# Splitting expert weights a whole slab at a time, with the products of the low parts queued one slab later

## The chip, the cores and the metric

The kernel runs on one core of one Trainium2 chip. The metric is the device time of one execution in microseconds (us); smaller is better. Three runs of the kernel before have a median of 2082.76 us (2081.35 to 2083.7).

## What is computed

The reference is a two-layer trunk over 256 latent tokens of width 1024, with 256 context tokens beside them. Layer 0 has a pooling and attention mixer and a dense SwiGLU, layer 1 a gated DeltaNet mixer and a SwiGLU of eight experts, of which each token uses two. The change lies in the experts:

```python
D_MODEL = 1024; SEQ = 256; N_EXPERTS = 8; TOP_K = 2; D_EXPERT = 3584

def swiglu(h, w1, w3, w2):
    return (jax.nn.silu(h @ w1) * (h @ w3)) @ w2

logits = jnp.matmul(t, router, preferred_element_type=jnp.float32)
top_v, top_i = lax.top_k(logits, TOP_K)
gates = jax.nn.softmax(top_v, axis=-1)
combine = jnp.sum(jax.nn.one_hot(top_i, N_EXPERTS) * gates[..., None], axis=1)
for e in range(N_EXPERTS):
    y = y + combine[:, e:e + 1] * swiglu(t, w1[e], w3[e], w2[e])
```

All data are fp32. The expert weights, 3 x 8 x 1024 x 3584 numbers, are 352 MB, and the kernel reads all of them.

## The kernel before

**Products in two parts.** TensorE multiplies in a reduced format (F32R), so each operand is split: a high part, which is the operand copied into F32R, and a low part, the rest. `split_w` (L235) does this for 1024 columns of weights: ScalarE (ACT) writes the high part `whi` (L238), VectorE (DVE) subtracts it from the raw weights and writes `wlo` (L239). Each of the two has a ring of three tiles in the pool `wp`. The same function serves every weight matrix of the kernel, also in the first 1090 us, before the experts. A product is then high by high, low by high and high by low (`mm3w`, L243 to L246).

**Slabs.** Weights come from HBM in slabs of 128 x 2048 numbers, 1 MB each, one DMA per slab, all issued by SyncE (SP) from `load` (L232) or `slab` (L1524). The experts have 8 x 7 units of work (expert, chunk of 512 hidden columns), and a unit has six slabs: four for `up` (two halves of the contraction for w1 and w3 each) and two for `down`, so 336 slabs. A slab waits in one of nine raw buffers, three from the pool `rawp` and six (`NR`) from `rw2`, taken in rotation; four more slabs use spare tiles (`spare`) that later hold other data. A raw buffer is free again when both halves of its slab are split, so the last reader is the subtraction at L239.

**Large and small experts.** The expert of index 0 and the three with the most tokens are large (128 slots, high and low part of the tokens as two weights of TensorE: three matmuls per block of 128 x 512, L244 to L246). The four with the fewest tokens are small (64 slots, high and low part side by side in 128 columns: two matmuls per block, L1804 and L1806 in `up`, L1859 and L1861 in `down`). So a slab of a large expert has 12 matmuls of 512 columns and one of a small expert 8. `units` (L1923) interleaves a chunk of a small and a chunk of a large expert.

**Order of one unit.** `up(c)` (L1789) does the first two slabs, then `turn` of the previous unit (L1821: the activations are transposed, or for a small expert folded at L1828, split by ACT and DVE at L1830 to L1841), then the other two slabs, and then reads out its sums (L1813 to L1818). After it comes `down` of the previous unit (L1844). The products of a half slab stand in the code directly behind its split. The order in the code is a priority: for each engine the language draws up the order of its instructions when the program is built, and at run time every engine works its list strictly in that order, waiting on semaphores.

**Where it starts and ends.** The first slabs are requested while layer 1 still runs. `route_large` and `route_small` gather the tokens of an expert. `finish` (L1866) spreads an expert's output over the tokens. After the last unit come the last norm and the output (L1998 to L2002).

```python
        n = turn[0] - 1 - sum(j < turn[0] for j in spare)
        return load(src, rawp if n % (NR + 3) < 3 else rw2)
```

Of the kernel before, what the change touches and what calls it, by code (L numbers as in the profile page):

```python
# [18 lines left out]
P = 128  # L19
# [149 lines left out]
def trunk(ctx, tc, I, out, dbg=None, stop=None):  # L169
# [12 lines left out]
    def psA():  # L182
        return pa.tile([P, 512], F32, tag="A", name="psA")
# [304 lines left out]
    with ExitStack() as mx:  # L488
# [131 lines left out]
        def softmax(qt, kv):  # L620

            lat = qt < 2
            k0 = 0 if lat else SEQ
            nk = T - k0
            r64 = slice(64 * kv, 64 * kv + 64)
            if kv == 0:
                prs = []
                for tag in ("whi", "wlo"):
                    pr = wp.tile([P, 1024], F32, tag=tag, name="pr")
                    prs += [pr[:, 0:512], pr[:, 512:1024]]  # L630
            else:
                prs = [w2() for g in range(4)]
            nm = sp.tile([P, 4], F32, tag="nm", name="nm")
            l4 = sp.tile([P, 4], F32, tag="l4", name="l4")
            mx_ = sp.tile([P, 4, 2], F32, tag="mx", name="mx")
            for g in range(4):
                h = 4 * kv + g
                n1 = nm[:, g:g + 1]
                ps = psA()
                TE.matmul(ps[:, :nk], qT[g][r64, qt * P:(qt + 1) * P], kT[0][r64, k0:], start=True, stop=True)  # L640
                if lat:
                    V.tensor_tensor_reduce(ps[:, :SEQ], ps[:, :SEQ], amask[:, qt, :], 1.0, -3e38, OP.add, OP.max,
                                           mx_[:, g, 0:1])
                V.tensor_reduce(mx_[:, g, 1:2], ps[:, nk - SEQ:nk], axis=AX.X, op=OP.max)
                V.tensor_scalar(n1, mx_[:, g, 1:2], -0.125, nsink[:, h:h + 1], op0=OP.mult, op1=OP.min)
                if lat:
                    V.tensor_scalar(n1, mx_[:, g, 0:1], -0.125, n1, op0=OP.mult, op1=OP.min)
                S.activation(prs[g][:, :nk], ps[:, :nk], AF.Exp, bias=n1, scale=0.125, accum_out=l4[:, g:g + 1])
                yield True
            es = sp.tile([P, 4], F32, tag="es", name="es")  # L650
            V.tensor_add(es, sinkb[:, 4 * kv:4 * kv + 4], nm)
            S.activation(es, es, AF.Exp)
            V.tensor_add(l4, l4, es)
            V.reciprocal(l4, l4)
            for g in range(4):
# [943 lines left out]
    def m2():  # L1599
        return tm.tile([P, 512], F32, tag="m2", name="m2")  # L1600
# [163 lines left out]
    def route_small(x):  # L1764
# [11 lines left out]
        for h in range(2):  # L1776
# [2 lines left out]
                TE.transpose(ps[:, col(i)], f(oh[:, i % 2, 2 * h + i // 2].rearrange("p a s -> p (a s)")), ident)  # L1779
            S.activation(oTs[:, 2 * h:2 * h + 2].rearrange("p e t s -> p (e t s)"), ps, AF.Copy)  # L1780

    def expert(w, into, gain, first=False):


# [3 lines left out]

        def up(c, ahead=None, raws=None, between=None):  # L1789
            h1, h3 = psA(), psA()  # L1790
            for kh in range(2):
                if kh and between:
                    between()
                raw1, raw3 = raws or [slab(w(n, c, kh)) for n in ("moe1", "moe3")]
                raws = None
                for q in range(2):
                    if ahead:
                        next(ahead, None)
                    for raw_, ps in ((raw1, h1), (raw3, h3)):
                        wh, wl = ready.pop(0) if ready else split_w(raw_[:, q * 1024:(q + 1) * 1024])  # L1800
                        ks = [(4 * kh + 2 * q + kk, slice(kk * 512, (kk + 1) * 512)) for kk in range(2)]
                        if small_:
                            for k, s in ks:
                                TE.matmul(ps, into.x(k), wh[:, s], start=k == 0, stop=False)  # L1804
                            for k, s in ks:
                                TE.matmul(ps, into.x(k), wl[:, s], start=False, stop=k == KD - 1)  # L1806
                        else:
                            for k, s in ks:
                                mm3w(ps, into.x[:, k, 0, :], into.x[:, k, 1, :], wh[:, s], wl[:, s], k == 0,
                                     k == KD - 1)  # L1810
            if small_:
                hs = [m2(), m2()]
                S.activation(hs[0], h1, AF.Copy)  # L1813
                S.activation(hs[1], h3, AF.Copy)
                return hs
            sg = m2()
            S.activation(sg, h1, AF.Silu)
            V.tensor_mul(sg, sg, h3)  # L1818
            return sg

        def turn_(sg):  # L1821
            ps = psA()
            gh = mo.tile([P, 512], F32R, tag="gh", name="gh")
            if small_:
                for i in range(2):
                    for b in range(4):
# [17 lines left out]
        def down(c, ghl, between=None):  # L1844
            gh, gl = ghl
            if not y:
                y.extend([psB(), psB()])
            for fh_ in range(2):
                if fh_ and between:
                    between()  # L1850
                raw_ = slab(w("moe2", c, fh_))
                for q in range(2):
                    b = 2 * fh_ + q
                    wh, wl = split_w(raw_[:, q * 1024:(q + 1) * 1024])
                    start, stop = c == 0 and b == 0, c == NCH - 1 and b == 3
                    halves = [slice(n * 512, (n + 1) * 512) for n in range(2)]
                    if small_:
                        for n, s in enumerate(halves):
                            TE.matmul(y[n], gh[:, col(b)], wh[:, s], start=start, stop=False)  # L1859
                        for n, s in enumerate(halves):  # L1860
                            TE.matmul(y[n], gh[:, col(b)], wl[:, s], start=False, stop=stop)  # L1861
                    else:
                        for n, s in enumerate(halves):
                            mm3w(y[n], gh[:, col(b)], gl[:, col(b)], wh[:, s], wl[:, s], start, stop)

        def finish():  # L1866
            yhl_ = mo.tile([P, 2, D], F32R, tag="hl", name="yhl_")
# [67 lines left out]
    last = None  # L1935
    ending, aheads = [], []
    count = NE * NCH
    for n, (into, c) in enumerate(units()):
        if n == 0:
            sg = into.up(c, ahead, raws0)  # L1940
            for _ in ahead:
                pass
            gains()
            sort()
            aheads = [route_small(xs_)]
            next(aheads[0])
        else:
            got = []
            sg = into.up(c, between=lambda: got.append(last.turn(last.sg)))
            if ending:  # L1950
                next(ending.pop(), None)
            if n == count - 1:
                last.down(last.c, got.pop(), lambda: got.append(into.turn(sg)))
            else:
                last.down(last.c, got[0])
            if last.c == NCH - 1:
                ending.append(last.finish())
                next(ending[0])
        if n == 1:
            sorted_experts()  # L1960
        if into in large and c == 0 and into is not large[-1]:
# [4 lines left out]
                if next(aheads[0], 0) == 0:  # L1966
                    aheads.pop(0)
        last = into
        last.sg, last.c = sg, c
    last.down(last.c, got[0])  # L1970
    for _ in last.finish():
        pass

# [2 lines left out]
    with tc.If(n_most > CAP):  # L1976
        with tc.For_i(0, NE) as e:
# [11 lines left out]
            expert(lambda n, c, s: I[n][bass.ds(e, 1), c, s].rearrange("o p f -> (o p) f"), into,  # L1989
                   lambda t: one[:, t, 1:2])  # L1990
            for c in range(NCH):
                into.down(c, into.turn(into.up(c)))
            for _ in into.finish():
                pass

# [24 lines left out]
```

## Time and profile before

| what | value |
|---|---|
| runs, median | 2082.76 us (2081.35 to 2083.7) |
| the profiled execution, its own time | 2079.91 us |
| its span, first to last instruction | 2078.1 us |
| mean granted TensorE clock | 0.978 of full speed |
| read from HBM in all | 516.67 MB |

The profile is of one execution. "Busy" is the time in which an engine executes; DMA share is the mean busy share of the 16 DMA engines. PEld is TensorE's weight load, which runs beside its matmuls; the matmuls' ends are modelled, so that consecutive ones overlap in the profile and their distance, start to start, says what one costs. In the list of waits, "A <- B: us, times" is the idle time of an engine just before instruction A that B ended. The tile names are the program's, and `psA` and `psB` are the two PSUM pools.

### The profile page before, as it was taken

How to read it: one execution, taken by the hardware profiler on the slowest of the kernel's cores; microseconds unless marked ns; L12 is line 12 of the kernel's file. 1: busy time of each engine (PE TensorE's matmuls, PEld its weight loads, DVE VectorE, ACT ScalarE, POOL GpSimd, SP SyncE). 2: the span in 40 equal slices, each digit the busy share in tenths (PEclk: the TensorE clock that was granted, in tenths of full speed). 3: DMA queues.
4: the chain of work that ended last, by engine and by line, in shares of the span. 5: the costliest groups of instructions: out<-in, count | busy, mean ns of one | idle time of the engine just before them, and what ended most of it. 6: DMA issues, size and time to landing. Idle time of an engine off the chain costs nothing. (4 is left out here: it accounts for less than half of the span.)

```text
span 2078.1 us, 29337 instructions
## 1 busy us (share of the span) xinstructions
PE 1941.4 (93%) x10425; PEld 1523.2 (73%) x10425; DVE 1601.4 (77%) x2522; ACT 1372.7 (66%) x2231; POOL 117.8 (6%) x163
## 2 busy tenths in 40 slices
PE   6999999999999899899979999999999999999996
PEld 3747677788888778898857877676767676766774
DVE  3475755576778687786659998889898888889897
ACT  5254654455666656645448887778777778777775
POOL 0000000000011214213000000000000000000000
PEclk9999999999999999999979999999999999999999
DMA  9352577744545233113147999898989899999993
GB/s 354 142 194 82 192 261 261 268 158 158 192 159 187 96 139 132 41 63 121 64 183 276 374 386 363 338 348 356 387 348 357 331 383 369 355 364 352 366 381 121
DMA packets 74074, 519.70 MB, mean 250 GB/s; under 512 B 9456, under 2 KB 9616, under 8 KB 11584
## 3 DMA queue, kind: packets, MB, share of 16 engines
q1 hardware_dynamic: 72864, 515.51, 65.4%
q0 software_dynamic: 1056, 2.24, 0.5%
q8 instruction: 84, 1.38, 0.3%
q14 instruction: 70, 0.57, 0.1%
HBM read 516.67 MB, written 1.05 MB: 249 GB/s over the span
## 5 line engine op out<-in xcount | busy, mean ns | idle before, releaser
L239 DVE TENSOR_TENSOR wlo<-raw,whi 128x1024 fp32r<-128x1024 f32 x878 | 1042.9, 1227 | 174.7 <-ACT whi L238 164.8
L238 ACT ACTIVATE whi<-raw 128x1024 fp32r<-128x1024 f32 x878 | 903.1, 1056 | 245.2 <-PE psA L245 98.6
L246 PE MATMUL psA<-wlo,xl 128*128 128x512 f32 x448 | 179.1, 400 | 8.4 <-DVE wlo L239 8.4
L244 PE MATMUL psA<-whi,xl 128*128 128x512 f32 x448 | 182.7, 409 | 2.5 <-ACT whi L238 1.6
L245 PE MATMUL psA<-whi,xl 128*128 128x512 f32 x448 | 176.4, 394 | 0.0
L1806 PE MATMUL psA<-wlo,xs 128*128 128x512 f32 x448 | 148.1, 412 | 14.4 <-DVE wlo L239 14.4
L1804 PE MATMUL psA<-whi,xs 128*128 128x512 f32 x448 | 147.3, 408 | 7.9 <-ACT whi L238 7.9
L244 PE MATMUL psB<-whi,gh 128*128 128x512 f32 x312 | 124.3, 399 | 0.1
L245 PE MATMUL psB<-whi,gl 128*128 128x512 f32 x312 | 123.4, 395 | 0.0
L246 PE MATMUL psB<-wlo,gh 128*128 128x512 f32 x312 | 112.0, 407 | 4.5 <-DVE wlo L239 4.1
L1806 PEld LDWEIGHTS psA<-wlo,xs 128*128 128x128 f32 x448 | 76.1, 188 | 52.3 <-DVE wlo L239 40.7
L787 PE MATMUL psB<-fx,whi 128*128 128x512 f32 x308 | 111.9, 402 | 0.7 <-DVE w L446 0.7
L787 PE MATMUL psA<-fx,whi 128*128 128x512 f32 x308 | 111.2, 399 | 0.6 <-DVE w L793 0.6
L246 PEld LDWEIGHTS psA<-wlo,xl 128*128 128x128 f32 x448 | 84.7, 189 | 35.2 <-DVE wlo L239 17.4
L1804 PEld LDWEIGHTS psA<-whi,xs 128*128 128x128 f32 x448 | 80.9, 189 | 35.8 <-ACT whi L238 21.2
L244 PEld LDWEIGHTS psA<-whi,xl 128*128 128x128 f32 x448 | 84.5, 189 | 26.0 <-ACT whi L238 10.5
L245 PEld LDWEIGHTS psA<-whi,xl 128*128 128x128 f32 x448 | 84.8, 189 | 17.1 <-DVE xl L1744 0.3
L788 PE MATMUL psB<-fx,wlo 128*128 128x256 f32 x352 | 91.7, 281 | 0.0
L788 PE MATMUL psA<-fx,wlo 128*128 128x256 f32 x352 | 91.6, 281 | 0.0
L1861 PE MATMUL psB<-wlo,gh 128*128 128x512 f32 x224 | 77.2, 426 | 15.0 <-DVE wlo L239 15.0
L264 POOL TENSOR_TENSOR rstd<-rstd,mhalf 128x1 f32<-128x1 f32 x17 | 13.5, 798 | 1358.4 <-DVE ss L1554 1002.4
L249 PE MATMUL psB<-jx,whi 128*128 128x256 f32 x256 | 78.1, 305 | 3.2 <-DVE glast L446 3.2
(519 smaller groups left out, 3853.0 us busy)
## 6 DMA issues: line engine op xcount, KB each, us to landing
raw<-in_moe SPq DMA_DIRECT2D x336, 1024.0 KB, 7.2
raw<-in_ffn SPq DMA_DIRECT2D x66, 1024.0 KB, 4.9
raw<-in_l_mod SPq DMA_DIRECT2D x48, 1024.0 KB, 6.4
raw<-in_w_qkvz SPq DMA_DIRECT2D x24, 1024.0 KB, 4.9
raw<-in_w_out SPq DMA_DIRECT2D x8, 1024.0 KB, 4.9
raw<-in_w_in SPq DMA_DIRECT2D x5, 1024.0 KB, 9.8
w<-in_l_post POOLq DMA_DIRECT2D x8, 256.0 KB, 4.9
x<-in_x SPq DMA_DIRECT2D x2, 512.0 KB, 5.0
```

The source lines that it names most:

```text
L238: S.activation(hi, src, AF.Copy)
L239: V.tensor_sub(lo, src, f(hi))
L244: TE.matmul(ps, ah, bh, start=start, stop=False)
L245: TE.matmul(ps, al, bh, start=False, stop=False)
L246: TE.matmul(ps, ah, bl, start=False, stop=stop)
L249: TE.matmul(ps, ah, bh, start=start, stop=False)
L264: G.tensor_tensor(r, r, mhalf[:, 0:n], op=OP.pow)
L787: TE.matmul(ps2, wh[:, c], hilo[:, k], start=k == 0, stop=False)
L788: TE.matmul(ps2[:, 0:SEQ], wl[:, c], hi[:, k], start=False, stop=False)
L1804: TE.matmul(ps, into.x(k), wh[:, s], start=k == 0, stop=False)
L1806: TE.matmul(ps, into.x(k), wl[:, s], start=False, stop=k == KD - 1)
L1861: TE.matmul(y[n], gh[:, col(b)], wl[:, s], start=False, stop=stop)
```

## The change

- `split_w` allocates its high and low part as one tile of `wp` (tag "w", three buffers) in place of two tiles with rings of their own. Memory stays as it was. The attention tile `pr` follows.
- In the experts, a new `split_slab` splits all 2048 columns with one ACT and one DVE instruction. The high part goes to a buffer of `rawp` (three of 2048 columns), the low part to one of `wp` (three of 2048 columns).
- Raw slabs now use the six buffers of `rw2` alone; the spare tiles stay.
- `later` holds back the products of the low parts: in the order of the code, those of a slab come behind the products of the high part of the next slab. The reading out of a unit's sums (`hidden`) and the start of `finish` are held back with them.
- The first two slabs of the first unit keep the old way (two halves of 1024).

```diff
     def split_w(src, n=1024):
-        hi = wp.tile([P, n], F32R, tag="whi", name="whi")
-        lo = wp.tile([P, n], F32R, tag="wlo", name="wlo")
+        both_ = wp.tile([P, 2, n], F32R, tag="w", name="w")
+        hi, lo = both_[:, 0], both_[:, 1]
...
-        n = turn[0] - 1 - sum(j < turn[0] for j in spare)
-        return load(src, rawp if n % (NR + 3) < 3 else rw2)
+        return load(src, rw2)
+
+    def split_slab(src):
+
+        hi = rawp.tile([P, 2048], F32R, tag="raw", name="whi")
+        lo = wp.tile([P, 2048], F32R, tag="w", name="wlo")
+        S.activation(hi, src, AF.Copy)
+        V.tensor_sub(lo, src, f(hi))
+        return hi, lo
...
-        spare[NR + 6 + j] = lambda tag=tag: mo.tile([P, 2048], F32, tag=tag, name="raw")
+        spare[NR + 3 + j] = lambda tag=tag: mo.tile([P, 2048], F32, tag=tag, name="raw")
...
+    pending = []
+
+    def later(*work):
+
+        for g_ in pending[:]:
+            g_()
+        pending[:] = work
...
+                for name, ps in (("moe1", h1), ("moe3", h3)):
+                    wh, wl = split_slab(slab(w(name, c, kh)))
+                    ks = [(4 * kh + i, slice(i * 512, (i + 1) * 512)) for i in range(4)]
+                    for k, s in ks:
+                        high(ps, wh, k, s)
+
+                    def lows_(ps=ps, wl=wl, ks=ks):
+                        for k, s in ks:
+                            low(ps, wl, k, s)
+
+                    later(lows_)
...
+            pending.append(hidden)
...
-                raw_ = slab(w("moe2", c, fh_))
-                for q in range(2):
-                    b = 2 * fh_ + q
-                    wh, wl = split_w(raw_[:, q * 1024:(q + 1) * 1024])
...
+                wh, wl = split_slab(slab(w("moe2", c, fh_)))
+                parts_ = [(2 * fh_ + q, n, slice(q * 1024 + n * 512, q * 1024 + (n + 1) * 512))
+                          for q in range(2) for n in range(2)]
+                for b, n, s in parts_:
+                    TE.matmul(y[n], gh[:, col(b)], wh[:, s], start=c == 0 and b == 0, stop=False)
+                    if not small_:
+                        TE.matmul(y[n], gl[:, col(b)], wh[:, s], start=False, stop=False)
+
+                def lows_(wl=wl, parts_=parts_):
+                    for b, n, s in parts_:
+                        TE.matmul(y[n], gh[:, col(b)], wl[:, s], start=False, stop=c == NCH - 1 and b == 3)
+
+                later(lows_)
...
             if last.c == NCH - 1:
-                ending.append(last.finish())
-                next(ending[0])
+                pending.append(lambda last=last: begin_end(last))
```

## Rows read from the trace of the kernel before

**Rows 1.** The page, part 1: busy time and share of the span.
```profile
PE 1941.4 (93%) x10425; PEld 1523.2 (73%) x10425; DVE 1601.4 (77%) x2522; ACT 1372.7 (66%) x2231; POOL 117.8 (6%) x163
```

**Rows 2.** Windows: length, busy us by engine, then PEclk, DMA share, GB/s.
```profile
0.00:1090.00 1090.00, 1020.73 (x6325) 829.68 (x6326) 726.99 (x1618) 598.14 (x1299) 116.71 (x161) 0.97 0.46 164
1130.00:2040.00 910.00, 859.61 (x3818) 646.89 (x3817) 809.25 (x803) 720.88 (x857) 0.00 (x0) 1.00 0.93 361
1828.00:1858.00 30.00, 28.36 (x126) 20.90 (x125) 26.12 (x26) 23.71 (x28) 0.00 (x0) 1.00 1.00 407
```

**Rows 3.** Groups of instructions by shape, 1130 to 2040 us.
```profile
L239 DVE TENSOR_TENSOR wlo<-raw,whi 128x1024 fp32r<-128x1024 f32 x628 | 734.4, 1222 | 62.3 <-ACT whi L238 58.6 <-PE psB L1861 0.5
L238 ACT ACTIVATE whi<-raw 128x1024 fp32r<-128x1024 f32 x629 | 641.2, 1056 | 94.7 <-PE psA L245 61.3 <-PE psB L245 10.0 <-DVE wlo L239 9.8
...
L1835 DVE TENSOR_TENSOR gh<-m,gh 128x256 fp32r<-128x256 f32 x26 | 10.9, 420 | 0.0
...
L1834 ACT ACTIVATE gh<-m 128x256 fp32r<-128x256 f32 x26 | 10.5, 404 | 0.5 <-DVE m L1831 0.5
```

**Rows 4.** Who waited for whom, 1130 to 2040 us: total, times, longest.
```profile
ACT whi L238 <- PE psA L245: 61.3, 77, 1.7
DVE wlo L239 <- ACT whi L238: 58.6, 94, 1.5
ACT m L1830 <- PE psA L1828: 54.7, 26, 2.3
PEld psA L1806 <- DVE wlo L239: 40.2, 71, 1.6
...
PEld psB L1861 <- DVE wlo L239: 33.8, 46, 2.2
PEld psB L246 <- DVE wlo L239: 20.2, 56, 1.9
PEld psA L1804 <- ACT whi L238: 19.0, 42, 1.8
PEld psA L246 <- DVE wlo L239: 16.5, 23, 1.0
...
PEld psA L244 <- ACT whi L238: 10.2, 25, 0.9
```

**Rows 5.** Waits of SP's queue, 1130 to 2040 us.
```profile
SPq L232 <- DVE wlo L239: 710.0, 301, 7.4
```

**Rows 6.** The tile raw, 1130 to 2040 us: time from issue to landing.
```profile
DMA to landing us min/median/max: 4.7/7.2/10.0
```

**Rows 7.** Timeline of ACT and of DVE, around 1510 us: splits back to back.
```profile
1509.89 6.09 ACT L238 ACTIVATE whi<-raw 128x1024 fp32r<-128x1024 f32 x6
...
1511.29 6.90 DVE L239 TENSOR_TENSOR wlo<-raw,whi 128x1024 fp32r<-128x1024 f32 x6
```

**Rows 8.** Timeline of PE, around 1500 us: a fold, and the order and distance of products.
```profile
1497.61 1.22 PE L1828 MATMUL psA<-fold,m 128*128 128x64 f32 x10
...
1506.89 0.39 PE L244 MATMUL psA<-whi,xl 128*128 128x512 f32 x1
1507.12 0.39 PE L245 MATMUL psA<-whi,xl 128*128 128x512 f32 x1
1507.35 0.39 PE L244 MATMUL psA<-whi,xl 128*128 128x512 f32 x1
1507.57 0.39 PE L246 MATMUL psA<-wlo,xl 128*128 128x512 f32 x1
```

**Rows 9.** Timeline of SP, 1000 to 1160 us: the first requests for expert slabs.
```profile
1009.82 43.35 SPq L232 DMA_DIRECT2D raw<-in_moe  x9
1067.17 0.83 SPq L1528 DMA_DIRECT2D raw<-in_moe  x2
1089.44 69.17 SPq L232 DMA_DIRECT2D raw<-in_moe  x21
```

**Rows 10.** Who waited for whom, 0 to 1090 us.
```profile
ACT whi L238 <- PE psB L250: 28.6, 15, 4.1
...
PEld psA L249 <- ACT whi L238: 5.8, 3, 3.1
```

**Rows 11.** Timeline of DVE, 2015 to 2079 us: the last splits.
```profile
2057.58 3.50 DVE L239 TENSOR_TENSOR wlo<-raw,whi 128x1024 fp32r<-128x1024 f32 x3 [0.41 <-ACT whi L238]
```

More of the change, by code (lines that the diff above doesn't have):

```diff
@@ L626, in softmax @@
             if kv == 0:
[L627 to L630, printed above, removed]
+                pr = wp.tile([P, 4, 512], F32, tag="w", name="pr")
+                prs = [pr[:, g] for g in range(4)]
             else:
@@ L1790, in up, with high, low @@
             h1, h3 = psA(), psA()
+            def high(ps, wh, k, s):
+                if small_:
+                    TE.matmul(ps, into.x(k), wh[:, s], start=k == 0, stop=False)
+                else:
+                    TE.matmul(ps, into.x[:, k, 0, :], wh[:, s], start=k == 0, stop=False)
+                    TE.matmul(ps, into.x[:, k, 1, :], wh[:, s], start=False, stop=False)
+            def low(ps, wl, k, s):
+                TE.matmul(ps, into.x(k) if small_ else into.x[:, k, 0, :], wl[:, s], start=False, stop=k == KD - 1)
             for kh in range(2):
@@ L1793, in up @@
                     between()
-                raw1, raw3 = raws or [slab(w(n, c, kh)) for n in ("moe1", "moe3")]
-                raws = None
-                for q in range(2):
-                    if ahead:
+                if raws and not kh:
+                    for q in range(2):
                         next(ahead, None)
[L1799 to L1821, printed above, removed]
+                        for raw_, ps in zip(raws, (h1, h3)):
+                            wh, wl = ready.pop(0) if ready else split_w(raw_[:, q * 1024:(q + 1) * 1024])
+                            for kk in range(2):
+                                s = slice(kk * 512, (kk + 1) * 512)
+                                high(ps, wh, 2 * q + kk, s)
+                                low(ps, wl, 2 * q + kk, s)
@@ new lines, in up @@
+                    next(ahead, None)
+                    next(ahead, None)
+                    continue
+                for name, ps in (("moe1", h1), ("moe3", h3)):
[7 more added lines that the diff above has]
+                    later(lows_)
@@ L1822, in turn_, with hidden @@
+            def hidden():
+                if small_:
+                    into.sg = [m2(), m2()]
+                    S.activation(into.sg[0], h1, AF.Copy)
+                    S.activation(into.sg[1], h3, AF.Copy)
+                else:
+                    into.sg = m2()
+                    S.activation(into.sg, h1, AF.Silu)
+                    V.tensor_mul(into.sg, into.sg, h3)
+            pending.append(hidden)
+        def turn_(sg, final=False):
             ps = psA()
-            gh = mo.tile([P, 512], F32R, tag="gh", name="gh")
+            gh = (tm if final else mo).tile([P, 512], F32R, tag="m2" if final else "gh", name="gh")
@@ L1850, in down @@
                     between()
-                raw_ = slab(w("moe2", c, fh_))
-                for q in range(2):
-                    b = 2 * fh_ + q
-                    wh, wl = split_w(raw_[:, q * 1024:(q + 1) * 1024])
[L1855 to L1864, printed above, removed]
+                wh, wl = split_slab(slab(w("moe2", c, fh_)))
[9 more added lines that the diff above has]
+                later(lows_)
         def finish():
@@ L1937, in trunk, with begin_end @@
     count = NE * NCH
+    def begin_end(into):
+        ending.append(into.finish())
+        next(ending[0])
     for n, (into, c) in enumerate(units()):
         if n == 0:
-            sg = into.up(c, ahead, raws0)
+            into.up(c, ahead, raws0)
+            later()
             for _ in ahead:
@@ L1948, in trunk @@
             got = []
-            sg = into.up(c, between=lambda: got.append(last.turn(last.sg)))
+            into.up(c, between=lambda: got.append(last.turn(last.sg)))
+            if n == count - 1:
+                last.down(last.c, got.pop(), lambda: got.append(into.turn(into.sg, True)))
+            else:
+                last.down(last.c, got[0])
             if ending:
                 next(ending.pop(), None)
[L1952 to L1955, printed above, removed]
             if last.c == NCH - 1:
-                ending.append(last.finish())
-                next(ending[0])
+                pending.append(lambda last=last: begin_end(last))
         if n == 1:
@@ L1968, in trunk @@
         last = into
-        last.sg, last.c = sg, c
+        last.c = c
     last.down(last.c, got[0])
+    later()
+    while ending:
+        for _ in ending.pop():
+            pass
     for _ in last.finish():
@@ L1991, in trunk @@
             for c in range(NCH):
-                into.down(c, into.turn(into.up(c)))
+                into.up(c)
+                later()
+                into.down(c, into.turn(into.sg))
+                later()
             for _ in into.finish():
```

## The prediction

> **What bounds the kernel now.** The page's first part makes TensorE look like the bound: PE is busy 93% of the span [rows 1]. That is an average over two stages, so the windows come next. In the first 1090 us PE is busy 1020.7 us and the other engines about two thirds of the time or less, and transfers take a share of 0.46 [rows 2]: that stage belongs to PE. The change lies in the other stage. From 1130 to 2040 us, DVE is busy 809 of 910 us, the transfers' share is 0.93 and PE reads 860 us [rows 2], but PE's figure is inflated by the modelled ends: products start 0.227 us apart (0.68 us over three steps) while the profile gives each 0.39 us [rows 8].
>
> So I reckon per slab. The 628 subtractions of this window [rows 3] are 314 slabs, and 910 us over 314 is **2.90 us per slab**. Against it stand four floors:
>
> - Transfers: 1.0486 MB at 407 GB/s, which the window from 1828 us holds for 30 us at a share of 1.00 [rows 2], is 2.58 us. At the stage's mean rate, 361 GB/s divided by its share of 0.93, it is 2.70 us.
> - DVE: 809 us over 314 is 2.58 us, of which 734.4 / 314 = 2.34 is the splitting [rows 2, 3].
> - PE: large slabs have 12 products, small ones 8, so 10 x 0.227 = 2.27. A pair of units (12 slabs) has 16 folds of 0.12 each [rows 8], 0.16 per slab. I add 0.1, an estimate, for transposes, gathers and `finish`: 2.53 us.
> - ACT: 721 / 314 = 2.30 us [rows 2].
>
> Nothing is full; three engines and the transfers stand within 15% of one another, and 0.3 us per slab is lost between them. The list of waits shows where [rows 4]. ACT cannot copy because a half slab's tile is still in use by PE (61 us behind L245). DVE, which then waits for ACT, loses 59 us. ACT waits 55 us at the fold (26 times), and DVE 32 us behind it, in the rest of its 101 idle us (910 - 809). PE's weight loads wait for low parts, 40.2 + 33.8 + 20.2 + 16.5 = 111 us in four groups, but for high parts only 29 us in two. It is a ring too short for its round trip: three halves are 1.5 slabs. While one half is used, two are ahead, 2 x 1.45 = 2.9 us, and refilling one costs 1.06 us on ACT and 1.22 us on DVE [rows 3] plus the handovers. SP's queue tells which side of the raw buffers is late: it waits 710 us in all for L239 to free one [rows 5]. Transfers wait for compute, not the reverse.
>
> **The change, part by part.**
>
> *One split per slab.* DVE takes 420 ns for 256 columns and 1222 for 1024 [rows 3], 1.044 ns per column, so 2048 columns should take 1222 + 1069 = 2291 ns. ACT by its own two rows (404 and 1056) takes 1056 + 869 = 1925 ns. Six half subtractions back to back take 6.90 us instead of 6 x 1.222 = 7.33, each start 0.09 earlier [rows 7]; if that overlap remains, one whole subtraction costs 2.20. Against 2.34 per slab now, DVE saves 0.05 to 0.14 us, 16 to 44 us over the stage; ACT, 2.04 now [rows 3], saves 0.12 or more. I count both at nothing in the sum: at the cadence I arrive at, transfers at their mean rate (2.70) stand above DVE's 2.44 to 2.53. If transfers keep 407 GB/s instead, some of it comes on top; that end belongs to the range.
>
> *Low products one slab later, rings of three whole slabs.* Two slabs ahead are 5.8 us against 1.93 + 2.29 = 4.2 us of refilling, so the loop has 1.6 us to spare where it had about half a microsecond. The subtraction also leaves PE's way: while DVE works on a slab, PE has its high products (4 or 8, 0.9 to 1.8 us) and the low ones of the slab before. What falls is DVE's wait for ACT, 58.6 us [rows 4]. It cannot fall below nothing, and a gain of all 58.6 would need that no turn disturbs the flow. I take three quarters, **-44 us**, because the waits are short (1.5 us at most) and the spare 1.6 us covers one of that size but not two in a row. The 32 us at the fold I leave: the fold keeps its place in the middle of `up`, and ACT still works strictly in order. The 111 us of weight loads are no separate term, since PE's waits are the same lost time seen from the other end. -44 us over 314 slabs is 0.14, so the cadence becomes 2.76, just above the transfers' 2.70: what is late next is a raw slab.
>
> *Six raw buffers for nine.* A buffer now lives 9 x 2.90 = 26 us: 7.2 in flight [rows 6], some 3.5 under the split, about 15 us lying loaded. Six at 2.76 are 16.6 us: 7.2 in flight, 1.93 + 2.29 + handovers = 4.5 under the split, 5 us lying loaded, nearly two slabs. Nothing in the sum; the rival below is its price. At the start, 2 + 9 + 2 = 13 slabs are requested before the first release at 1089 us (two of them before the window shown) [rows 9]; after the change it is 10. Three slabs fewer cost 0 as long as compute is the late side, and 3 x 2.58 = 8 us if transfers bind from there to the end. I take 0, as SP's waits point that way.
>
> *Deferred read-outs.* `hidden` runs behind the next high products, 4 to 8 x 0.227 us later, and is used half a unit later (some 8 us): 0, with that time as cover. Without it PE would wait at the turn, one ACT step.
>
> *One tile for high and low in the first 1090 us.* A copy now also waits for the last low product of its slot, one product more (about 0.2 us). ACT waits for PE's high product there, 15 times at L250 for one group, but PE for ACT's high part only 5.8 us in 3 times [rows 10]. PE has the cover. Between 0 and +8 us; I take +1.
>
> *The end.* The last slab is split by 1.93 + 2.29 = 4.2 us in place of 1.06 and two chasing subtractions (the last three take 3.50 us, 1.17 each [rows 11]), 3.4 us, and two more products of 0.23 come behind it: +1.
>
> **Sum:** -44 + 1 + 1 = -42 us. The profiled execution took 2079.9 us, 2.9 below the median of the runs; it goes to 2038, and the median, 2082.8, to **2041 us**.
>
> One rule of the Trainium skill touches a floor. "HBM Reference", Specifications, puts a core that streams alone at about 425 GB/s; the highest rate in the rows here is 407. By 425 a slab would take 2.47 us, transfers would never be the late side, and the DVE saving could be added, an estimate of 2000 to 2025 us. The forecast stays with the rows.
>
> **The rivals.**
>
> *The transfers starve (slower).* Six buffers leave about two loaded slabs. The longest wait of SP for a release is 7.4 us [rows 5], and a request takes 4.7 us at least to land [rows 6], so a gap of that length leaves the engines dry for 2.7 us. The transfers' idle share is 7% of 910 = 64 us already, with nine. If each of the 26 folds [rows 4] adds 2.7 us, it is +70; at every second one +35: 2118 us. It decides from gaps over some 5 us, longer than the two loaded slabs last. For it: the share is 0.93 now. Against it: the gaps are DVE's stalls, which the change shortens. 14%.
>
> *The whole copy becomes the wait (slower).* PE waits for a high part 67 times in the two groups shown [rows 4]. Each would be 0.87 us longer (1.93 against 1.06), +58; the low parts' waits that disappear are worth at most half as much, because only some reach PE's products: about +23, 2106 us. "Perfetto Trace Analysis", Optimizing Scalar/DVE Operations, of the Trainium skill has the rule behind it: where these engines are not saturated but cause bubbles elsewhere, smaller instructions finish work sooner. The change does the opposite; no run here shows yet which holds. 9%.
>
> *The order was there already.* PE's list is not the code's: L244, L245, L244, L246 [rows 8] runs another block's high product before the low one. If the list already sets low products back wherever that helps, only longer instructions and a longer ring are left, of which the ring's first half slab would serve: -10 us, 2073. 12%, half of it too small to see.
>
> *All floors reached.* Cadence 2.62: -0.28 x 314 = -88, 1995 us. Three servers this close to one another rarely run without loss. 7%.
>
> **How the numbers follow.** The forecast has 58%; its own range, from half of the 58.6 us to all of them and 7 us of DVE's saving, is 2018 to 2058 us. A measurement of this kernel can tell about 0.2%, 4 us, from no change. Faster: 58 + 7 + 6 = 71%; same 8%, which is the other half of the third rival and the edge of its neighbours; slower 21%, the two slower rivals less that edge. The range of 8 in 10 reaches to 2006 below, which leaves out the last rival, and to 2106 above, which leaves out most of starving transfers and half of the copy's case.
>
> **What would show it.** Right: one L239 of 2.2 to 2.3 us per slab, ACT 1.93; DVE's wait for `whi` near 15 us; weight loads' waits for `wlo` almost gone; a DMA share of 0.96 or more in the stage at 375 to 385 GB/s; the first 1090 us within 2 us. Wrong: a share under 0.93 with SP still waiting for L239 means starving raw buffers; weight loads waiting over 70 us for `whi` means the copy; an unchanged `wlo` wait means that the order was there already; a first stage longer by over 8 us means the joint tile.

## The result and the profile after

The change made the kernel slower: a median of 2098.2 us (2097.0 to 2102.9, four runs) against 2082.6, a ratio of 1.0079 with a 95% interval of 1.0062 to 1.0097. The forecast was 2041 us and faster.

The profiled execution has a span of 2096.5 us, 18.4 more than before. The first stage has no part in it. SP's timeline after the change, from 960 us on, has the first request that waits for a freed slab buffer at the same moment as before, 1089.0 against 1089.4 us [rows 9], with 2 + 6 + 2 slabs ahead of it in place of 13:

```profile
979.62 0.81 SPq L1526 DMA_DIRECT2D raw<-in_moe  x2
1041.25 14.30 SPq L232 DMA_DIRECT2D raw<-in_moe  x6
1063.11 1.61 SPq L1526 DMA_DIRECT2D raw<-in_moe  x2
1089.02 70.30 SPq L232 DMA_DIRECT2D raw<-in_moe  x22
```

The loss is in the experts. The windows after the change (length, busy time of PE, PEld, DVE, ACT and POOL, then granted clock, DMA share, GB/s), to set against [rows 2]:

```profile
0.00:1090.00 1090.00, 1016.52 (x6306) 824.27 (x6307) 723.19 (x1614) 597.61 (x1298) 113.50 (x161) 0.97 0.45 161
1130.00:2040.00 910.00, 832.33 (x3759) 645.41 (x3758) 769.01 (x477) 657.90 (x532) 0.00 (x0) 1.00 0.95 355
```

The same 910 us hold 308 slabs now (the groups below), 314 before: 2.95 us per slab in place of 2.90. DVE is idle 141 us where it was idle 101, ACT 252 where it was 189. Per slab every engine is busy for less time than before (DVE 2.50 us against 2.58, ACT 2.14 against 2.30), and yet the stage is longer. The groups of instructions by shape in this window, against [rows 3], say that the new instructions cost what was expected of them, 2286 ns (2291 expected) and 1907 ns (1925):

```profile
L1535 DVE TENSOR_TENSOR wlo<-raw,whi 128x2048 fp32r<-128x2048 f32 x308 | 693.7, 2286 | 100.3 <-ACT whi L1534 95.1 <-PE psA L1814 1.9 <-PE psB L1895 1.6
L1534 ACT ACTIVATE whi<-raw 128x2048 fp32r<-128x2048 f32 x308 | 572.5, 1907 | 7.5 <-PE psA L1811 3.1 <-issue 2.9 <-PE psB L1891 1.5
```

The list of waits after the change, 1130 to 2040 us (total, times, longest), shows what took the place of what in [rows 4]:

```profile
ACT m L1864 <- PE psA L1862: 105.6, 25, 5.0
DVE wlo L1535 <- ACT whi L1534: 95.1, 97, 1.4
ACT gh L1874 <- PE psA L1872: 56.9, 22, 3.2
PEld psA L1814 <- DVE wlo L1535: 56.1, 74, 1.4
PEld psB L1889 <- ACT whi L1534: 45.2, 60, 1.1
PEld psB L1895 <- DVE wlo L1535: 37.7, 27, 1.8
DVE m L1865 <- ACT m L1864: 35.7, 21, 1.9
ACT m L1850 <- PE psA L1814: 29.7, 24, 1.2
...
ACT m L1846 <- PE psA L1814: 22.6, 25, 2.3
ACT m L1847 <- PE psA L1814: 13.2, 23, 1.1
ACT whi L1534 <- PE psA L1811: 3.1, 5, 0.9
```

L1862 is the fold of a small expert (L1828 before), L1864 the ACT instruction that reads it, L1872 and L1874 the same of a large expert, L1846 to L1850 the reading out of a unit's sums. ACT's wait for a free tile, 61.3 us at one product alone before [rows 4], is 3.1 us: the longer rings did what they were to do. But ACT's wait at the fold's read-out went from 54.7 to 105.6 us, and the five read-outs above wait 105.6 + 56.9 + 29.7 + 22.6 + 13.2 = **228 us**. One period of the stage shows how. ACT's timeline after the change:

```profile
1498.74 7.32 ACT L1534 ACTIVATE whi<-raw 128x2048 fp32r<-128x2048 f32 x4
1511.00 0.39 ACT L1864 ACTIVATE m<-psA 128x256 f32<-128x256 f32 x1 [4.93 <-PE psA L1862]
1511.28 1.91 ACT L1534 ACTIVATE whi<-raw 128x2048 fp32r<-128x2048 f32 x1
1513.08 0.41 ACT L1868 ACTIVATE gh<-m 128x256 fp32r<-128x256 f32 x1
1514.73 0.60 ACT L1850 ACTIVATE m<-psA 128x512 f32<-128x512 f32 x1 [1.24 <-PE psA L1814]
1515.22 9.12 ACT L1534 ACTIVATE whi<-raw 128x2048 fp32r<-128x2048 f32 x5
```

After four copies in a row ACT is done at 1506.1 us and stands for 4.93 us at L1864, because PE gets to the fold only at 1509. The next copy is behind it in ACT's list, and in the 9 us from 1506 to 1515 ACT makes one copy. DVE's timeline of the same stretch follows it with three gaps, 1.84 + 1.38 + 1.31 us:

```profile
1511.42 0.42 DVE L1865 TENSOR_TENSOR m<-m,psA 128x256 f32<-128x256 f32 x1 [1.84 <-ACT m L1864]
1513.22 2.29 DVE L1535 TENSOR_TENSOR wlo<-raw,whi 128x2048 fp32r<-128x2048 f32 x1 [1.38 <-ACT whi L1534]
...
1517.16 2.29 DVE L1535 TENSOR_TENSOR wlo<-raw,whi 128x2048 fp32r<-128x2048 f32 x1 [1.31 <-ACT whi L1534]
```

### The profile page after: what moved, and what is told of

The parts are those of the page before. It is cut to its first block, busy times and chain, and to the rows that moved or that the text cites. A ratio compares the mean times of both kernels' runs of the same rounds, so it can differ in the third digit from the quotient of the medians.

```text
span 2096.5 us, 28061 instructions
## 1 busy us (share of the span) xinstructions
PE 1925.1 (92%) x10425; PEld 1529.6 (73%) x10425; DVE 1573.0 (75%) x2188; ACT 1318.7 (63%) x1897; POOL 114.6 (5%) x163
## 3 DMA queue, kind: packets, MB, share of 16 engines
q8 instruction: 84, 1.38, 0.3%
## 5 line engine op out<-in xcount | busy, mean ns | idle before, releaser
L1535 DVE TENSOR_TENSOR wlo<-raw,whi 128x2048 fp32r<-128x2048 f32 x334 | 752.6, 2286 | 105.8 <-ACT whi L1534 98.6
L1534 ACT ACTIVATE whi<-raw 128x2048 fp32r<-128x2048 f32 x334 | 621.5, 1908 | 12.7 <-PE psA L1811 7.0
L239 DVE TENSOR_TENSOR w<-raw,w 128x1024 fp32r<-128x1024 f32 x210 | 260.7, 1242 | 95.5 <-ACT w L238 92.7
L238 ACT ACTIVATE w<-raw 128x1024 fp32r<-128x1024 f32 x210 | 221.5, 1057 | 136.3 <-PE psA L246 34.7
L1814 PE MATMUL psA<-wlo,xs 128*128 128x512 f32 x448 | 132.9, 416 | 26.9 <-DVE wlo L1535 25.4
L1889 PEld LDWEIGHTS psB<-whi,gh 128*128 128x128 f32 x448 | 80.9, 188 | 66.9 <-ACT whi L1534 47.5
L1814 PEld LDWEIGHTS psA<-wlo,xs 128*128 128x128 f32 x448 | 76.4, 188 | 69.5 <-DVE wlo L1535 58.5
L1895 PEld LDWEIGHTS psB<-wlo,gh 128*128 128x128 f32 x448 | 81.8, 188 | 56.2 <-DVE wlo L1535 38.7
L1814 PE MATMUL psA<-wlo,xl 128*128 128x512 f32 x440 | 119.7, 394 | 0.0
L785 PE MATMUL psB<-fx,w 128*128 128x512 f32 x308 | 113.6, 407 | 1.8 <-DVE w L446 1.8
L785 PE MATMUL psA<-fx,w 128*128 128x512 f32 x308 | 111.4, 400 | 0.8 <-DVE w L791 0.6
L786 PE MATMUL psB<-fx,w 128*128 128x256 f32 x352 | 92.4, 283 | 0.0
L1814 PEld LDWEIGHTS psA<-wlo,xl 128*128 128x128 f32 x440 | 80.7, 188 | 15.8
L786 PE MATMUL psA<-fx,w 128*128 128x256 f32 x352 | 91.6, 281 | 0.0
```

Of the source, the lines that this page charges most:

```text
L785: TE.matmul(ps2, wh[:, c], hilo[:, k], start=k == 0, stop=False)
L786: TE.matmul(ps2[:, 0:SEQ], wl[:, c], hi[:, k], start=False, stop=False)
L1814: TE.matmul(ps, into.x(k) if small_ else into.x[:, k, 0, :], wl[:, s], start=False, stop=k == KD - 1)
L1889: TE.matmul(y[n], gh[:, col(b)], wh[:, s], start=c == 0 and b == 0, stop=False)
L1895: TE.matmul(y[n], gh[:, col(b)], wl[:, s], start=False, stop=c == NCH - 1 and b == 3)
```

## The experiments

The theories that the runs were to tell apart: **read-outs in ACT's list** (ACT stands at an instruction that reads what PE has not done yet, and copies for which everything is there wait behind it); **the whole copy** (PE waits for long instructions); **the raw buffers** (six are too few); **the order of the low products**; **the joint tile**. Every kernel computes the whole of the layer. Each was timed in turns with the kernel before on the same chip; the kernel before had a median of 2080 to 2083 us in every series, so times of different series can be compared to within a few us.

**e1: the joint tile alone.** The kernel before with `split_w` as changed, nothing else.

```diff
-        hi = wp.tile([P, n], F32R, tag="whi", name="whi")
-        lo = wp.tile([P, n], F32R, tag="wlo", name="wlo")
+        both_ = wp.tile([P, 2, n], F32R, tag="w", name="w")
+        hi, lo = both_[:, 0], both_[:, 1]
```

> The kernel before with only the joint tile for high and low part in the first 1090 us and in the experts' half slabs. If the joint tile costs the first stage: the first expert slab after the spare ones is requested later and the total rises by 5 to 15 us over before. If it is free, as the trace after the change suggests (first release at 1089.0 us against 1089.4): within 4 us of before.

Measured: 2098.7 us, ratio 1.0081 (1.0056 to 1.0106). The first release came at 1093.3 us, 4 later than before; the rest of the 17 us is in the experts, whose half slabs use the same ring here. Its list of waits there:

```profile
ACT w L238 <- PE psA L246: 54.7, 74, 1.7
ACT m L1828 <- PE psA L1826: 47.5, 25, 2.1
ACT w L238 <- PE psA L1804: 20.1, 51, 1.5
ACT w L238 <- PE psB L1859: 19.5, 29, 2.9
ACT w L238 <- PE psB L246: 13.9, 47, 0.5
```

The copies now wait for the low products (L246, and L1804 and L1859 of the small experts in this kernel), 54.7 + 20.1 + 19.5 + 13.9 = 108 us. Before, they waited 61.3 + 10.0 us for L245, 4.6 for L1859 and 9.8 for DVE, 86 us (all but the third in [rows 3]). Holding the high part back by a product or two costs a ring of 1.5 slabs about 13 us in this stage. It is not the cause in the changed kernel, whose expert slabs have rings of their own again; what it shows is how tight the ring before was. Neither expectation was right: the cost was there, but mostly not in the first stage.

**e2: half instructions.** The changed kernel; `split_slab` makes two copies and two subtractions into the same tiles.

```diff
-        S.activation(hi, src, AF.Copy)
-        V.tensor_sub(lo, src, f(hi))
+        for q in range(2):
+            s = slice(q * 1024, (q + 1) * 1024)
+            S.activation(hi[:, s], src[:, s], AF.Copy)
+            V.tensor_sub(lo[:, s], src[:, s], f(hi[:, s]))
```

> The changed kernel, with each slab split in two copies and two subtractions of 1024 columns into the same whole-slab tiles; buffers and order of the code as changed. Theory of the whole copy (long instructions make PE wait): the waits of PE and its weight loads for whi (about 45 + 24 us after the change) halve and the total falls by 20 us or more, to 2078 or less. Theory of the in-order read-out (ACT stands at the turn's read-out until PE gets there, with the next slab's copy behind it): ACT still waits some 100 us at the small expert's read-out, and the total stays within 8 us of 2098. Theory of the missing raw buffers: no change either.

Measured: 2103.8 us, ratio 1.0112 (1.0096 to 1.0129). ACT waits 100.1 us at the fold's read-out and 80.3 at the large expert's. The waits of PE and its weight loads for `whi` did not halve: they are 92 us in all, 73 in the changed kernel. The theory of the whole copy falls for the changed kernel as it stands. The run shows one thing more: DVE's wait for `whi` fell from 95.1 to 26.6 us and the time did not fall with it, so a wait of DVE that goes away is not by itself a gain.

**e3: low products at once.** The changed kernel with `later(lows_)` replaced by what is pending and then `lows_()`, in `up` and in `down`.

> The changed kernel with the low products directly behind their own slab's high products (read-outs as deferred as before this edit). If putting them one slab later is what keeps the loss from being larger: 10 us or more slower than 2098, since the weight loads wait the whole subtraction (2.29 us) for each slab. If the order is what costs, because it holds the low parts' buffers longer and makes the read-outs late: 10 us or more faster. In-order read-out theory: ACT's wait at the small read-out stays near 100 us, total within 8 us.

Measured: 2095.6 us, ratio 1.0076 (1.0059 to 1.0093); ACT's wait at the fold is 123.0 us. So neither a gain nor the loss comes from the new place of the low products.

**e4: the turn behind the next two copies.** In the code of `up`, both slabs of the second half are split before `between()` (the turn), and the turn's ACT instructions are tied in ACT's list behind the second copy. The tie sets the order of the list alone and adds no wait.

```diff
                 if kh and between:
-                    between()
+                    for name in ("moe1", "moe3"):
+                        split_[name] = split_slab(slab(w(name, c, kh)))
+                    with tc.issue_after(copies[-1].ins):
+                        between()
```

> The changed kernel with both slabs of the second half of up split ahead of the turn in the code, and the turn's ACT instructions placed behind the second of these copies in ACT's list. In-order read-out theory: the wait at the small expert's read-out (105.6 us in 25) falls by about one copy each, to 60 us or less, DVE's wait for whi falls with it, and the total falls by 25 to 50 us, to 2050 to 2075. Theory of the whole copy or of the missing raw buffers: the time is within 8 us of 2098, or above it because the turn comes later.

Measured: 2099.4 us, ratio 1.0102 (1.0078 to 1.0126): no gain. The wait at the fold (L1869 here) fell from 105.6 to 57.0 us as expected, but others grew, and DVE's wait for `whi`, which was to fall, rose from 95.1 to 135.4. Its list of waits, 1130 to 2040 us:

```profile
DVE wlo L1535 <- ACT whi L1534: 135.4, 58, 5.1
ACT m L1855 <- PE psA L1815: 79.6, 24, 3.3
ACT m L1869 <- PE psA L1867: 57.0, 22, 2.8
PEld psB L1894 <- DVE gh L1874: 56.9, 23, 2.9
...
ACT m L1851 <- PE psA L1815: 49.3, 25, 3.2
```

L1855 and L1851 read out a unit's sums (29.7 and 22.6 us in the changed kernel). With the fold moved back, they stood next in the list, again ahead of the copies, and PE now waited for `gh`. Either the theory was wrong, or half of the read-outs had been moved.

**e5: all of them.** As e4, and every pair of slabs, in `down` too, is split ahead of its products; what `later` runs (the read-out of the sums, the start of `finish`) is tied behind the second copy of the pair.

```diff
+    def behind():
+        return tc.issue_after(copies[-1].ins)
...
-        for g_ in pending[:]:
-            g_()
+        with behind() if copies else ExitStack():
+            for g_ in pending[:]:
+                g_()
```

> The changed kernel with both copies of a pair of slabs ahead of what reads out, everywhere: the turn's ACT instructions behind the second copy of up's second half, the read-out of a unit's sums behind the second copy of down. So ACT is two slabs ahead of PE when it comes to a read-out. If the order of ACT's list is what costs: ACT's waits at read-outs (228 us in five groups after the change) fall below 120, DVE's wait for whi below 50, and the total is 2040 to 2075. If the order only moves the wait, because the loop over ACT, DVE and PE at a turn is the cost: the sum of ACT's waits stays above 180 us, PE waits for gh instead, and the total stays within 10 us of 2098.

Measured: **2022.2 us**, ratio 0.9730 (0.9711 to 0.9749), 76 us under the changed kernel, beyond the expected range. The five read-outs that waited 228 us now wait 73 (52.8 at the fold, 12.2, 5.2, 2.1 and 0.3 at the rest, in 850 us), and DVE's wait for `whi` is 20.6 us (another 33.1 us of its idle time stand behind L1879, an ACT instruction of the turn). One period of ACT in this run:

```profile
1446.61 1.92 ACT L1534 ACTIVATE whi<-raw 128x2048 fp32r<-128x2048 f32 x1 [0.56 <-DMA raw<-in_moe]
1449.11 1.92 ACT L1534 ACTIVATE whi<-raw 128x2048 fp32r<-128x2048 f32 x1 [0.58 <-DMA raw<-in_moe]
1453.70 0.39 ACT L1875 ACTIVATE m<-psA 128x256 f32<-128x256 f32 x1 [2.67 <-PE psA L1873]
1453.99 1.91 ACT L1534 ACTIVATE whi<-raw 128x2048 fp32r<-128x2048 f32 x1
1455.79 0.40 ACT L1879 ACTIVATE gh<-m 128x256 fp32r<-128x256 f32 x1
1456.12 1.92 ACT L1534 ACTIVATE whi<-raw 128x2048 fp32r<-128x2048 f32 x1
1457.94 0.58 ACT L1861 ACTIVATE m<-psA 128x512 f32<-128x512 f32 x1
1459.30 7.42 ACT L1534 ACTIVATE whi<-raw 128x2048 fp32r<-128x2048 f32 x4 [0.77 <-ACT m L1861]
```

Two copies wait for a transfer, which none does in the lists of before and after. Such waits are small, 4.1 us in nine over the stage, but they show that slabs now come late at times. And the windows of this run, with PE busy 69.79 of 70 us and transfers at a share of 1.01 in the second:

```profile
1130.00:1980.00 850.00, 820.69 (x3816) 660.54 (x3815) 775.64 (x489) 674.14 (x542) 0.00 (x0) 1.00 0.98 387
...
1420.00:1490.00 70.00, 69.79 (x331) 57.17 (x330) 64.31 (x38) 56.35 (x43) 0.00 (x0) 1.00 1.01 419
```

**e6: six raw buffers alone.** The kernel before with every slab that has no spare tile loaded into `rw2`.

```diff
-        n = turn[0] - 1 - sum(j < turn[0] for j in spare)
-        return load(src, rawp if n % (NR + 3) < 3 else rw2)
+        return load(src, rw2)
```

> The kernel before with only the six raw buffers of rw2 for the slabs, the three of rawp idle; half slabs, separate rings and order as before. If six raw buffers starve the copies: ACT waits for DMA shows up in the list, SP's longest wait stays and the total rises by 15 us or more. If the raw buffers are in excess, as no copy waits for a transfer in any run so far: within 5 us of before (2080).

Measured: 2084.6 us, ratio 1.0020 (1.0011 to 1.0030). No copy waits for a transfer, and the window from 1130 to 2040 us moves 360 GB/s at a share of 0.93, as before [rows 2]. Three raw buffers fewer cost some 4 us, not 15: the second case.

**e7: the sums' read-outs alone.** As e5, the turn neither tied nor anything else done to it.

```diff
                 if kh and between:
-                    with behind():
-                        between()
+                    between()
```

> The kernel of the run e5 with the turn's ACT instructions left free, where the list of ACT puts them ahead of one copy more; the read-outs of a unit's sums stay behind down's copies. If it takes both places to be right: ACT's wait at the small turn (52.8 us in the run e5) comes back to some 100 us and the total lies half way, 2045 to 2085. If the read-outs of the sums alone carry the gain: within 8 us of 2022.

Measured: 2057.1 us, ratio 0.9881 (0.9850 to 0.9912), and ACT's wait at the fold is 111.6 us. It takes both places for the whole gain: the sums' read-outs, with the pairs split ahead, bring some 41 us of the 76 by themselves, and the turn some 35 more, though without the sums' read-outs (e4) it brought nothing.

**e8: e5 with low products at once**, by the edit of e3.

> The kernel of the run e5 with the low products directly behind their own slab's high products. If the deferral of the low products is worth something once ACT's list no longer holds the copies up: weight loads wait for wlo over 100 us (49 us in two groups in the run e5) and the total is 15 us or more above 2022. If not: within 5 us of 2022.

Measured: 2028.3 us, ratio 0.9745 (0.9726 to 0.9764). The interval overlaps that of e5: the expected 15 us are not there, and whether the deferral is worth a few us stays open. The weight loads wait 56 us for `wlo`, 47 in e5; in the changed kernel it is 94 and in e3, the same rings without the deferral, 133. So this wait fell with ACT's list in order, with the deferral or without.

**e9: ACT's list in the kernel before.** Half slabs, rings of three halves and nine raw buffers as before; the turn behind the second half copy of `up`'s second half, the sums' read-out behind the second half copy of `down`.

```diff
                 if kh and between:
-                    between()
+                    early = [split_w(r_[:, 0:1024]) for r_ in (raw1, raw3)]
+                    with behind():
+                        between()
...
+                if hidden:
+                    early = [split_w(raw_[:, q * 1024:(q + 1) * 1024]) for q in range(2)]
+                    with behind():
+                        hidden()
```

> The kernel before (half slabs, separate rings of three halves, nine raw buffers) with ACT's list ordered as in the run e5: the turn behind the second copy of up's second half, the read-out of the sums behind down's second copy, counted in half slabs. If the order of ACT's list alone is the cost in both kernels: 2030 to 2050. If the short ring of half slabs binds as well, as the 44 us of the prediction supposed: within 15 us of 2081, with ACT's waits for free tiles (L245 and the like, 85 us) as they were.

Measured: 2066.1 us, ratio 0.9930 (0.9912 to 0.9949). That lies at the edge of the second case, within 15 us of 2081, and it is still a clear gain: the order of the list alone is worth some 15 us in the kernel before, where the fold's wait falls from 54.7 to 28.0 us. Its waits for free tiles stay what they were (46.4 + 14.6 us for products and 21.0 for DVE, 82 us in a window of 850 us against 86 in 910):

```profile
ACT whi L238 <- PE psA L250: 46.4, 60, 1.7
ACT m L1842 <- PE psA L1840: 28.0, 24, 1.6
ACT whi L238 <- DVE wlo L239: 21.0, 42, 1.0
ACT whi L238 <- PE psB L250: 14.6, 46, 0.6
```

**e10: e5 with half instructions**, by the edit of e2.

> The kernel of the run e5 with two copies and two subtractions of 1024 columns per slab, into the same whole-slab tiles. If the single long instruction is worth its saved start-up (DVE 0.04 us per slab by 2.29 against 2 x 1.165, ACT more): a few us slower, 2024 to 2034. If smaller instructions free PE earlier and that counts: 2005 to 2018. If only the order and the rings matter: within 4 us of 2022.

Measured: 2007.6 us, ratio 0.9643 (0.9622 to 0.9663): 15 us under e5, where the same edit had if anything added 6 to the changed kernel. PE's weight loads wait 1.4 us for `wlo` in `down`, 9.4 in e5.

**e11: the remaining read-outs.** As e5; the routing's instructions tied behind `down`'s second copy and second subtraction, `finish`'s accumulation behind its second subtraction.

```diff
             if ending:
-                next(ending.pop(), None)
+                with behind_sub():
+                    next(ending.pop(), None)
...
-                if next(aheads[0], 0) == 0:
-                    aheads.pop(0)
+                with behind(), behind_sub():
+                    if next(aheads[0], 0) == 0:
+                        aheads.pop(0)
```

> The kernel of the run e5 with the remaining read-outs placed the same way: those of route_large and route_small behind down's second copy on ACT and its subtraction on DVE, and finish's accumulation behind down's second subtraction on DVE. In e5 the stretches with a finish or a route in them run at 354 to 358 GB/s, the others at 393 to 413. If the same in-order waiting causes that (ACT at hf 30 us, DVE at yacc 10 us): 5 to 20 us faster, 2002 to 2017. If these stretches are slow for PE's added work: within 4 us of 2022.

Measured: 1997.3 us, ratio 0.9598 (0.9582 to 0.9614), just under the expected range. A window with a finish or a route in it, in e5 (its other windows of 100 us run at 388 to 413 GB/s, but for the one from 1500 us with 358):

```profile
1300.00:1400.00 100.00, 92.76 (x439) 74.32 (x438) 87.05 (x62) 74.90 (x71) 0.00 (x0) 1.00 0.93 354
```

and e11:

```profile
1300.00:1400.00 100.00, 97.11 (x458) 78.33 (x457) 92.74 (x63) 80.92 (x74) 0.00 (x0) 1.00 0.97 375
```

The wait at `hf` fell from 30.3 to 10.3 us.

**e12: e11 with half instructions.**

> The two steps that helped together: all read-outs behind the next copies and subtractions (run e11, 1997) and two half copies and half subtractions per slab (run e10, 15 us under the run e5). If the gains are of different waits: 1980 to 1992. If both were drawn from the same waits, as transfers already run at a share of 0.98 to 0.99: within 5 us of 1997.

Measured: **1995.8 us**, ratio 0.9591 (0.9578 to 0.9604), 4% under the kernel before and the lowest of all. Its interval overlaps that of e11, so behind e11 the half instructions that gained 15 us on e5 gain nothing that can be told from noise: the second case, the two gains come from the same waits for the most part. The window of 700 us in the middle of its experts:

```profile
1200.00:1900.00 700.00, 693.85 (x3228) 560.97 (x3227) 677.53 (x680) 593.90 (x717) 0.00 (x0) 1.00 0.99 399
```

## Why the prediction was wrong

**The step that failed** is the sentence that left a term as it was: "The 32 us at the fold I leave: the fold keeps its place in the middle of `up`, and ACT still works strictly in order." Both halves of it are true, but the term did not stay as it was. ACT, no longer held up for tiles, comes to the fold's read-out earlier against PE and stands there longer: 105.6 us against 54.7. A second term failed with it, the deferred read-outs of a unit's sums, counted at 0 with half a unit as cover: their three lines waited 29.7 + 22.6 + 13.2 = 65.5 us, and e7 shows that their place in the list, with the pairs split ahead, is worth some 41 us. All five read-outs waited 228 us. Before, the same five (L1830, L1840, L1813, L1814 and L1817) waited 79 us: the first is in [rows 4], L1817 is not in the list of before, and the other three are

```profile
ACT m L1813 <- PE psA L1806: 12.6, 16, 0.8
ACT gh L1840 <- PE psA L1838: 10.8, 20, 1.1
...
ACT m L1814 <- PE psA L1806: 1.3, 4, 0.3
```

What ACT no longer waited for a tile (86 us before, under 5 after), it waited for PE's results, and 68 us more. I had priced a stall at an in-order queue as a fixed sum; it depends on how far the queue's engine is ahead of the one that it reads from. That the read-outs' places in ACT's list cost this time is shown by e5, e7 and e9. That it is the longer ring which brought ACT further ahead is argued by exclusion: the joint tile and the six raw buffers alone leave the fold's wait near what it was (47.5 us in e1, 57.5 in e6), and it stays without the long instructions (100.1, e2) and without the deferral of the low products (123.0, e3). The changed kernel with a shorter ring was not run.

**The ring's term, -44, was right in kind, and nothing of it arrived in the changed kernel.** The waits for a free tile went, as supposed, but DVE's wait for `whi`, which was to fall from 58.6 us to some 15, rose to 95.1, because the copies stood behind the read-outs. With the list ordered in both, e9 (2066) and e5 (2022) differ by 44 us, and DVE's wait for `whi` by 60.4 - 20.6 = 40 us. That this is the -44 of the sum to the microsecond is in part luck: the pair differs also in the joint tile, the raw buffers, the length of the instructions, the low products' place, and in how many copies the list puts ahead of a read-out (two halves in e9, two slabs in e5). With the list as the language drew it up, the same change cost 16 us. Put together: the list's order costs some 15 us in the kernel before (e9) and some 76 in the changed one (e5), and these 61 us more used up the 44 and left the loss of 16.

**The small terms.** One split per slab: 2286 and 1907 ns, as computed from the rows, and worth no more than the 6 us of e2 in the changed kernel (nothing assumed). Six raw buffers: 0 forecast, 4 us by e6. The rival of starving transfers falls: no copy in e6 or in the changed kernel waits for one. The joint tile in the first stage: +1 forecast; the changed kernel's first release is 0.4 us earlier, e1's 4 us later, so it lies within a few us. The end: from 2040 us on, the changed kernel runs 57 us where the kernel before ran 38; the six slabs that it has still to do there are 6 x 2.95 = 18 of these 19 us, so the end itself costs about the +1 that was forecast.

**The rival of the whole copy** came out on the right side of zero, and near the measured time, by luck: the cause was not its own. Its sign was to be weight loads waiting over 70 us for `whi`; they wait 47.9. Halving the instructions did not help the changed kernel (e2). (Its sum does not follow either: +58 less at most half as much leaves +29 or more, not +23.) The rule of the Trainium skill that stood beside it ("Perfetto Trace Analysis", Optimizing Scalar/DVE Operations: smaller instructions where these engines are not saturated but cause bubbles elsewhere) shows in one place only: no gain in e2, 15 us in e10 with two of the places of read-outs in order, nothing clear of noise in e12 with all of them. How long an instruction should be here thus depends on which waits are left.

**The third rival**, that the list already sets low products back, is half true: e3 and e8 give the deferral no more than a few us. Its other half, that a longer ring would bring only 10 us, does not fit the 44 us between e9 and e5. Its sign, an unchanged wait for `wlo`, was half given (94 us against 111) and would have pointed to the wrong cause.

None of the signs that I gave for a wrong prediction named this cause. The trace of before had it, though: 26 waits of ACT at L1830, of up to 2.3 us [rows 4], with a copy next in the list.

What stays open: e5 differs from the changed kernel by the ties, which add no wait, and by the place of each pair's splits in the code. For the turn the tie by itself is shown to carry some 35 us, once the sums' read-outs are in order (e7 lacks nothing else); for the sums' read-outs the splits' place was not run without the tie. Why the language drew up the list with the read-outs ahead of the copies was not looked into either.

## What to carry to other kernels

A longer ring between a copying engine and its consumer can move the next stall to whatever the copying engine reads back from that consumer: look at each read-out in its list and count how many copies stand ahead of it. Here two slabs ahead, with a ring of three, gave the gain; other numbers were not run. Try all such read-outs together before judging one, since a list that is free at one place can stop at the next: moved alone, the turn measured as nothing (e4), the sums' read-outs as 41 us (e7), and both as 76 (e5). A change that brings nothing may be right and wait for its order: here it was worth +16 us with the list as drawn up, and some -44 us with the list in order in both kernels (e9 to e5).

## What the runs showed of the hardware

The transfers' busy share is a poor gauge of how much room is left. It is 0.95 at 355 GB/s in the changed kernel, 0.93 at 361 before, 0.98 at 387 in e5. At 1.01 they moved 419 GB/s over 70 us, 1.0486 MB / 419 = 2.50 us per slab, below the floors of the prediction for transfers (2.58 and 2.70), DVE (2.58) and PE (2.53); only ACT's, 2.30, lies lower. "HBM Reference", Specifications, of the Trainium skill gives about 425 GB/s for a core that streams alone; the trace agrees within 2%, and the forecast's bound from 407 was too high.
